# Gate's row by transfers, into the weights of the last projection's second half, and shift columns in one operand: a change to a hybrid decoder layer

## The chip, the cores and the metric

The kernel runs on 1 core of a Trainium2 chip. A core has five engines with instruction queues of their own: TensorE (PE in the profile; its loads of stationary operands are PEld), VectorE (DVE), ScalarE (ACT), GpSimd (POOL) and SyncE (SP); the last two serve here mostly to issue transfers (DMAs). The metric is the device time of one execution in microseconds (us), lower is better.

## The reference

One sequence of 256 rows of 1024 features goes through one hybrid layer. Cut to what matters:

```python
mod = silu(c) @ ada_w + ada_b                       # nine rows of 1024
sh1, sc1, g1, sh2, sc2, g2, sh3, sc3, g3 = split(mod, 9)
u = modulate(rms_norm(h, norm_ffn1_w), sh1, sc1)    # x * (1 + scale) + shift
h = h + 0.5 * g1 * swiglu(u, ffn1_w_in, ffn1_w_out) # (silu(u @ w_gate) * (u @ w_up)) @ w_out
u = modulate(rms_norm(h, norm_mix_w), sh2, sc2)
h = h + g2 * hybrid_mixer(u, ...)                   # state space branch + retention, gated merge
u = modulate(rms_norm(h, norm_ffn2_w), sh3, sc3)
h = h + 0.5 * g3 * swiglu(u, ffn2_w_in, ffn2_w_out) # inner width 2816
return rms_norm(h, norm_final_w)
```

The change touches three things in it: `u` at the entry of the mixer and of the second SwiGLU (its shift), the row `0.5 * g3`, and the product with `ffn2_w_out` that the row multiplies.

## The kernel before

**Products.** Features lie on the 128 partitions and the 256 rows (T) along the columns, until the last projection, which is computed with the rows on the partitions. Every operand of a product is kept as two halves, `hi` (rounded to a shorter float) and `lo` (what is left over), and each fp32 product is three matmuls: hi·hi, hi·lo and lo·hi (`mm3`, L146 to L154, in the profile as L152, L153 and L154, or as L148 to L150 in a turned order).

**Weights.** `load` fetches 1 MB of weights through SP's queue into one of four stage tiles `wst`. `half` (L132 to L139) makes the two halves of 1024 columns in one of four tiles `wh`: ScalarE casts (L137), VectorE subtracts (L138). A stage tile is free for the fourth load after it once its last subtraction is done, a `wh` tile once its last matmul is done. So there is a chain from load to cast to subtraction to the first matmul that reads the low half (L154, where weights stand on the stationary side; L153 in the last projection, where they are the moving operand).

**Early projections.** Twice, at the entry of the mixer and of the second SwiGLU, `modulated` (L265) starts the next product through `early_project` before the rms factor and its application are done: the factor (`rs`, by `rstd`) is made while matmuls run on operands that lack it, and the four results are multiplied by it afterwards (L281). The shift can't go that way. It stands as extra columns T and T + 1 in the operand tiles `uh` and `ul` (written by `shift()` in `residual`), so that the products are 258 columns wide, and column T of each result is the bias that the shift makes; it is copied to `eb` (L280, 128x1). In the second SwiGLU the first result goes with that bias into a silu on ScalarE (L186 on `proj,eb`), and VectorE multiplies with the other (L975). Meanwhile TensorE goes on with the next 256 columns, whose weights are `wh_7775` and `wh_7802` in the order below.

**Second SwiGLU.** Eleven steps of 256 inner features fill `ah` and `al`, the halves of the activations. In the sixth, VectorE makes `g` (L987, 128x8: gate's 1024 numbers, eight to a partition) and a tile of eight diagonals (`diag`, L989). Two fp32 products of `diag` with ones (L993) spread the row over all partitions, and ScalarE copies it to `gb` (L995), 128x1024.

**Last projection.** Two passes of 512 output columns; each has six loads of up to four inner tiles, eleven `wh` tiles, and works for both row tiles (`ps[0]`, `ps[1]`). After pass 0 `gated` multiplies each result by the row (L1011), adds the residual stream `hN` (L1012), squares with a running sum on ScalarE (L1014) and multiplies by the final norm's weight (L1015). Pass 1 keeps its last six inner tiles: what stands in `ps[1]` is multiplied and added first (L1037, L1038), then row tile 0 is finished, then row tile 1 in two pieces of 256 columns, with `gated` after each. The last piece's square, the square root, the reciprocal (L1054), the scaling (L1061 on VectorE, L1063 on ScalarE) and the transfer to DRAM come after the last matmul.

What order the instructions have on each engine is set by a scheduler of the compiler's tile framework; only the mixer's part is written out in an order by hand (the strings of step names). A change of one instruction's form can therefore move others.

Of the kernel before, what the change touches and what calls it, by code (L numbers as in the profile page):

```python
# [18 lines left out]
P = 128  # L19
T = 256  # L20
# [62 lines left out]
def layer(ctx: ExitStack, tc: tile.TileContext, a, out, packing):  # L83
# [57 lines left out]
    def split_into(hi, lo, src):  # L141
        cast = act.copy(hi, src).ins  # L142
        dve.tensor_tensor(lo, src, hi.bitcast(F32), ALU.subtract)
        return cast

    def mm3(o, l, r, first, last, skip=False, turned=False):  # L146
        if turned:
            pe.matmul(o, l[1], r[0], start=False, stop=False, skip_group_check=skip)  # L148
            pe.matmul(o, l[0], r[0], start=False, stop=False, skip_group_check=skip)  # L149
            pe.matmul(o, l[0], r[1], start=False, stop=False, skip_group_check=skip)  # L150
            return
        pe.matmul(o, l[0], r[0], start=first, stop=False, skip_group_check=skip)  # L152
        pe.matmul(o, l[0], r[1], start=False, stop=False, skip_group_check=skip)  # L153
        pe.matmul(o, l[1], r[0], start=False, stop=last, skip_group_check=skip)  # L154

    def at(pair, *idx):
        return pair[0][idx], pair[1][idx]

    def wide_at(u, kt):
        return u[2][:, kt, :], u[3][:, kt, :]  # L160

    al = slice(None)

# [69 lines left out]

    def new_u():
        full = [sp.tile([P, KD, U_ROW], F32R, tag=n, name=nm(n), bufs=1) for n in ("uh", "ul")]
        return tuple(t[:, :, :T] for t in full) + tuple(t[:, :, :T + 2] for t in full)

    def u_tile(u, f, t, jsh):
        sh = modc[:, jsh, f:f + 1]
# [25 lines left out]
    def modulated(ha, u, jsh, w, cols, at_kt=1, c_next=None):  # L265
        rs = []
        ps = early_project(w, cols, u, at_kt, lambda: rs.append(rstd(sums, mean_m)))
        rs = rs[0]
        if c_next is not None:
            st = load(w, 0, KD, c_next, 256)  # L270
            ready.append(half(st[:, :, :P]))
        for f in range(KD):
            t = ha(f)
            dve.tensor_tensor(t, t, rs, ALU.mult)
            u_tile(u, f, t, jsh)
        if c_next is not None:
            ready.append(half(st[:, :, P:]))
        b = sp.tile([P, 4], F32, tag="eb", name=nm("eb"), bufs=1)
        for i in range(4):
            dve.tensor_copy(b[:, i:i + 1], ps[i][:, T:T + 1])  # L280
            dve.tensor_tensor(ps[i][:, :T], ps[i][:, :T], rs, ALU.mult)  # L281
        return [(ps[i][:, :T], b[:, i:i + 1]) for i in range(4)]

    def early_project(w, cols, u, at_kt, between):
        sts = [load(w, 0, KD, c0, 256) for c0 in cols]
        ps = [proj_ps().rearrange("p f t -> p (f t)") for _ in range(2)]
        ps += [misc_ps() for _ in range(2)]
        for kh in range(2):
            hv = [half(st[:, 4 * kh:4 * kh + 4, :]) for st in sts]
            for kk in range(4):  # L290
                kt = 4 * kh + kk
                if kt == at_kt:
                    between()
                for i in range(2):
                    for f in range(2):
                        mm3(ps[2 * i + f][:, :T + 2], at(hv[i], al, kk, slice(f * P, (f + 1) * P)),
                            wide_at(u, kt), kt == 0, kt == KD - 1)
        return ps

    def pair_halves(w, c0):  # L300
# [20 lines left out]
    def residual(jg, factor, am, ha, u, jsh):  # L321
        g = sp.tile([P, KD], F32, tag="g", name=nm("g"), bufs=2)
        dve.tensor_scalar(g, modc[:, jg, :], factor, None, ALU.mult)

        def shift():
            split_into(u[2][:, :, T:], u[3][:, :, T:],
                       modc[:, jsh, :].unsqueeze(2).broadcast_to([P, KD, 2]))

        def done(f, ps):
            if f == KD - 2:  # L330
                shift()
            dve.scalar_tensor_tensor(h[:, f, :], ps, g[:, f:f + 1], h[:, f, :], ALU.mult, ALU.add)
            square_add(f)
            act.activation(ha(f), h[:, f, :], AF.Copy, scale=am[:, f:f + 1])
            act.activation(u[0][:, f, :], h[:, f, :], AF.Copy, scale=am[:, f:f + 1])
            dve.tensor_tensor(u[1][:, f, :], ha(f), u[0][:, f, :].bitcast(F32), ALU.subtract)
        return done
# [626 lines left out]
    with tc.tile_pool(name=nm("fp"), bufs=1, reuse_waits="tile") as fp:  # L964
# [5 lines left out]
        for p2 in range(NF // 2):  # L970
            if p2 == 0:
                s = fp.tile([P, 2, T], F32, tag="s", name=nm("s"), bufs=2)
                for f in range(2):
                    lookup(s[:, f, :], first[f][0], AF.Silu, bias=first[f][1])
                    dve.scalar_tensor_tensor(s[:, f, :], first[2 + f][0], first[2 + f][1],  # L975
                                             s[:, f, :], ALU.add, ALU.mult)
                split_into(ah[:, 0:2, :], alo[:, 0:2, :], s)
            else:
                pg = pair_project(w1, p2 * 256, u, ready if p2 == 1 else None)
                pu = pair_project(w1, FFN + p2 * 256, u)  # L980
                swiglu(fp, pg, pu, ah, alo, 2 * p2)
            ada_next()
            if p2 == 1:
                nc.sync.dma_start(wf, a["norm_final_w"].broadcast_to([P, D]))
            if p2 == 5:
                g = sp.tile([P, KD], F32, tag="g", name=nm("g"), bufs=2)
                dve.tensor_scalar(g, modc[:, 8, :], 0.5, None, ALU.mult)  # L987
                diag = fp.tile([P, KD, P], F32, tag="diag", name="diag")
                dve.tensor_tensor(diag, ident.unsqueeze(1).broadcast_to([P, KD, P]),  # L989
                                  g.unsqueeze(2).broadcast_to([P, KD, P]), ALU.mult)  # L990
                for q in range(2):
                    ps = misc_ps()
                    pe.matmul(ps, ones, diag[:, 4 * q:4 * q + 4, :].rearrange("p f t -> p (f t)"),  # L993
                              start=True, stop=True)
                    act.copy(gb[:, q * 512:(q + 1) * 512], ps)  # L995
            if p2 == 6:
                for tt in range(2):
                    for q in range(2):
                        ps = misc_ps()
                        for f in range(4):  # L1000
                            pe.transpose(ps[:, f * P:(f + 1) * P],
                                         h[:, q * 4 + f, tt * P:(tt + 1) * P], ident)
                        act.copy(hN[:, tt, q * 512:(q + 1) * 512], ps)
# [3 lines left out]
        def gated(tt, ps, c0, n, i):  # L1007
            cs_ = slice(c0, c0 + n)
            t = fp.tile([P, 512], F32, tag="t", name=nm("t"), bufs=2)[:, :n]
            o = hN[:, tt, cs_]  # L1010
            dve.tensor_tensor(t, ps, gb[:, cs_], ALU.mult)  # L1011
            dve.tensor_tensor(t, o, t, ALU.add)  # L1012
            q = fp.tile([P, 512], F32, tag="q", name=nm("q"), bufs=1)[:, :n]
            act.activation(q, t, AF.Square, accum_out=ss[:, tt, i:i + 1])  # L1014
            dve.tensor_tensor(o, t, wf[:, cs_], ALU.mult)  # L1015

        for bi in range(2):
            c0, per, split = bi * 512, 4, NF - 6 if bi else NF
            ps = [proj_ps().rearrange("p f t -> p (f t)") for _ in range(2)]
            hvs = []  # L1020

            def product(o, tt, kt, part, first, last):
                mm3(o, at((ah, alo), al, kt, slice(tt * P, (tt + 1) * P)),
                    at(hvs[kt // 2], al, kt % 2, part), first, last)

            for k0 in range(0, NF, per):
                kn = min(per, NF - k0)
                st = load("ffn2_w_out", k0 * P, kn, c0, 512)
                hvs += [half(st[:, k2:k2 + 2, :], "alike") for k2 in range(0, kn, 2)]
                for kt in range(k0, min(k0 + kn, split)):  # L1030
                    for tt in range(2):
                        product(ps[tt], tt, kt, al, kt == 0, kt == (split if tt else NF) - 1)
            if not bi:
                for tt in range(2):
                    gated(tt, ps[tt], 0, 512, 0)
        t = fp.tile([P, 512], F32, tag="t", name=nm("t"), bufs=2)
        dve.tensor_tensor(t, ps[1], gb[:, 512:], ALU.mult)  # L1037
        dve.tensor_tensor(hN[:, 1, 512:], hN[:, 1, 512:], t, ALU.add)  # L1038
        for tt, q in ((0, None), (1, 0), (1, 1)):
            part = al if q is None else slice(q * T, (q + 1) * T)  # L1040
            o = ps[0] if q is None else proj_ps()[:, 0, :]
# [69 lines left out]
```

## Time and profile before

| | us |
|---|---|
| median of 3 runs | 828.91 (828.78 to 828.99) |
| profiled execution | 828.89 |
| its span in the trace | 826.8 |
| TensorE busy | 816.1 |
| VectorE busy | 666.9 |
| ScalarE busy | 511.0 |
| GpSimd busy | 10.3 |

The granted TensorE clock was 0.998 over the span. The profile comes from one execution: the span is what the trace covers, and 2.1 us lie around it. In rows of the timeline the columns are start, duration, engine, line, operation, output and inputs, the tile's shape and the count; in square brackets stands how long the engine was idle before, and what released it. A matmul's duration includes its way through the array, so matmuls overlap, and the distance from one start to the next is what one costs. Consecutive rows of one kind are joined into one with a count. Rows from the chain that ended last have start, duration, engine, tile and line.

### The profile page before, as it was taken

Reading aid. Unit: us, or ns where it says so; the run is one execution under the profiler, and the core shown is the slowest. Engines: PE = TensorE matmul, PEld = TensorE weight load, DVE = VectorE, ACT = ScalarE, POOL = GpSimd, SP = SyncE. Lnnn points to the kernel's source line nnn. Section 1 sums busy time; section 2 is a strip of 40 time slices with the busy share of each in tenths; the row PEclk is TensorE's granted clock in tenths of the full one; section 3 lists DMA queues with packets and bytes.
Section 4 is the critical chain, followed back from the end, with each engine's and each line's share of the span. In section 5 each row is a group of like instructions: output and inputs, shape, how many; then the busy total and the mean of one; then the engine's idle time right before and its main releaser. Section 6 shows DMA issues by size and latency. Waiting matters only on the chain.

```text
span 826.8 us, 15886 instructions
## 1 busy us (share of the span) xinstructions
PE 816.1 (99%) x6612; PEld 787.0 (95%) x6612; DVE 666.9 (81%) x999; ACT 511.0 (62%) x731; POOL 10.3 (1%) x21
## 2 busy tenths in 40 slices
PE   8999999999999999999999999999999999999996
PEld 7999999999999989999999999999999999999885
DVE  7999899977989988787898778977979985455464
ACT  6566454556898777765565569765568754545342
POOL 0000000000200010000000000000000000000000
PEclk9999999999999999999999999999999999999999
DMA  9998899855685465546657754654565695455521
GB/s 367 415 418 344 314 349 366 335 180 173 233 309 200 158 216 187 200 130 239 229 182 301 254 205 153 211 198 171 212 218 183 255 360 185 176 185 185 206 87 52
DMA packets 30299, 193.08 MB, mean 234 GB/s; under 512 B 3458, under 2 KB 4098, under 8 KB 9619
## 3 DMA queue, kind: packets, MB, share of 16 engines
q1 hardware_dynamic: 28370, 186.07, 61.6%
q0 software_dynamic: 1568, 5.28, 1.9%
q8 instruction: 52, 0.85, 0.4%
q10 hardware_dynamic: 288, 0.72, 0.3%
q14 instruction: 21, 0.16, 0.1%
HBM read 190.97 MB, written 1.08 MB: 232 GB/s over the span
## 4 chain that ended last, share of the span: by engine, by line
PE 90%; ACT 3%; DVE 3%; DMA 3%; issue 1%; SPq 0%; ACTq 0%
PE proj L154 25%; PE proj L153 25%; PE proj L152 25%; PE proj L149 2%; PE proj L150 2%; PE proj L148 2%; DMA wst<-in_ffn_w_in_dram 2%; ACT wh L411 1%; DMA ada<-in_ada_w_dram 1%; PE misc L754 1%; PE misc L898 1%; PE misc L223 1%; DVE wh L414 1%; DVE wh L138 1%; DVE ada L197 1%; PE misc L764 1%
## 5 line engine op out<-in xcount | busy, mean ns | idle before, releaser
L138 DVE TENSOR_TENSOR wh<-wst,wh 128x1024 fp32r<-128x1024 f32 (+1 forms) x262 | 316.8, 1213 | 108.4 <-ACT wh L137 107.5
L137 ACT CAST wh<-wst 128x1024 fp32r<-128x1024 f32 (+1 forms) x262 | 272.4, 1042 | 171.0 <-PE proj L154 132.2
L152 PE MATMUL proj<-uh,wh 128*128 128x256 f32 (+1 forms) x1096 | 304.5, 278 | 0.0
L153 PE MATMUL proj<-ul,wh 128*128 128x256 f32 (+1 forms) x1096 | 303.2, 277 | 0.0
L154 PE MATMUL proj<-uh,wh 128*128 128x256 f32 (+1 forms) x1096 | 303.2, 277 | 0.0
L153 PEld LDWEIGHTS proj<-ul,wh 128*128 128x128 f32 x1096 | 205.8, 188 | 0.4 <-issue 0.2
L152 PEld LDWEIGHTS proj<-uh,wh 128*128 128x128 f32 x1096 | 205.8, 188 | 0.3 <-ACT wh L137 0.2
L154 PEld LDWEIGHTS proj<-uh,wh 128*128 128x128 f32 x1096 | 205.8, 188 | 0.2 <-issue 0.2
L152 PE MATMUL proj<-s,wh 128*128 128x256 f32 x312 | 87.1, 280 | 0.2 <-ACT s L142 0.2
L154 PE MATMUL proj<-s,wh 128*128 128x256 f32 x312 | 86.4, 277 | 0.0
L153 PE MATMUL proj<-s,wh 128*128 128x256 f32 x312 | 86.2, 277 | 0.0
L152 PEld LDWEIGHTS proj<-s,wh 128*128 128x128 f32 x312 | 58.5, 188 | 0.6 <-ACT s L142 0.4
L153 PEld LDWEIGHTS proj<-s,wh 128*128 128x128 f32 x312 | 58.6, 188 | 0.2 <-issue 0.2
L154 PEld LDWEIGHTS proj<-s,wh 128*128 128x128 f32 x312 | 58.6, 188 | 0.0
L197 DVE SCALAR_TENSOR_TENSOR ada<-ada,cb 128x1024 f32<-128x1024 f32 x48 | 57.3, 1219 | 0.0
L148 PE MATMUL proj<-uh,wh 128*128 128x256 f32 x152 | 42.0, 276 | 0.0
L149 PE MATMUL proj<-uh,wh 128*128 128x256 f32 x152 | 42.0, 276 | 0.0
L150 PE MATMUL proj<-ul,wh 128*128 128x256 f32 x152 | 42.0, 276 | 0.0
L152 PE MATMUL proj<-ah,wh 128*128 128x256 f32 x152 | 42.0, 276 | 0.0
L153 PE MATMUL proj<-al,wh 128*128 128x256 f32 x152 | 42.0, 276 | 0.0
L154 PE MATMUL proj<-ah,wh 128*128 128x256 f32 x152 | 42.0, 276 | 0.0
L186 ACT ACTIVATE s<-proj 128x512 f32<-128x512 f32 x33 | 19.7, 598 | 34.6 <-PE proj L154 32.5
(274 smaller groups left out, 1372.8 us busy)
## 6 DMA issues: line engine op xcount, KB each, us to landing
wst<-in_mix_w_in_dram SPq DMA_DIRECT2D x52, 1024.0 KB, 4.9
wst<-in_ffn_w_in_dram SPq DMA_DIRECT2D x43, 1024.0 KB, 5.5
wst<-in_ffn_w_out_dram SPq DMA_DIRECT2D x18, 1024.0 KB, 4.9
ada<-in_ada_w_dram SPq DMA_DIRECT2D x16, 1024.0 KB, 8.4
wst<-in_ada_w_dram SPq DMA_DIRECT2D x12, 1024.0 KB, 5.0
ada<-in_ada_w_dram SPq DMA_DIRECT2D x16, 512.0 KB, 12.6
wst<-in_w_br_ssd_dram SPq DMA_DIRECT2D x8, 1024.0 KB, 5.0
wst<-in_w_br_ret_dram SPq DMA_DIRECT2D x8, 1024.0 KB, 4.9
```

The source lines that it names most:

```text
L137: act.copy(hi, v)
L138: dve.tensor_tensor(lo, v, hi.bitcast(F32), ALU.subtract)
L148: pe.matmul(o, l[1], r[0], start=False, stop=False, skip_group_check=skip)
L149: pe.matmul(o, l[0], r[0], start=False, stop=False, skip_group_check=skip)
L150: pe.matmul(o, l[0], r[1], start=False, stop=False, skip_group_check=skip)
L152: pe.matmul(o, l[0], r[0], start=first, stop=False, skip_group_check=skip)
L153: pe.matmul(o, l[0], r[1], start=False, stop=False, skip_group_check=skip)
L154: pe.matmul(o, l[1], r[0], start=False, stop=last, skip_group_check=skip)
L186: phase["uses"].append(act.activation(*args, **kw).ins)
L197: dve.scalar_tensor_tensor(st[:, i, :], st[:, i, :], 1.0, cb, ALU.mult, ALU.mult, accum_out=raw[:, j, f0 + i:f0 + i + 1])
L223: pe.matmul(ps[:, :T], mean, s, start=i == 0, stop=i == len(parts) - 1)
L411: act.copy(hw[0][j], wst[kt][:, j, :])
```

## The change

Three things, all in the second half of the kernel but for the first of two early projections:

1. Both halves of the shift go into the high operand: hi into column T of `uh`, lo into column T + 1. A new helper, `mm3_shifted`, multiplies 258 columns in the first and the third matmul and 256 in the second. The bias is the sum of two columns of each result, so the copy becomes a reduction.
2. Gate's row is no longer made by TensorE. Two transfers on GpSimd's queue write `g` to DRAM (1024 elements of 4 bytes, each to its place) and read it back to all partitions.
3. In pass 1 of the last projection VectorE multiplies each stage tile of weights by the row's second half, in place, before it is split; what `gated` and the piece before it multiplied there, falls away.

```diff
+    def mm3_shifted(o, l, u, kt, first, last):
+        pe.matmul(o[:, :T + 2], l[0], u[2][:, kt, :], start=first, stop=False)
+        pe.matmul(o[:, :T], l[0], u[1][:, kt, :], start=False, stop=False)
+        pe.matmul(o[:, :T + 2], l[1], u[2][:, kt, :], start=False, stop=last)
...
-            dve.tensor_copy(b[:, i:i + 1], ps[i][:, T:T + 1])
+            dve.tensor_reduce(b[:, i:i + 1], ps[i][:, T:T + 2], mybir.AxisListType.X, ALU.add)
...
-                        mm3(ps[2 * i + f][:, :T + 2], at(hv[i], al, kk, slice(f * P, (f + 1) * P)),
-                            wide_at(u, kt), kt == 0, kt == KD - 1)
+                        mm3_shifted(ps[2 * i + f], at(hv[i], al, kk, slice(f * P, (f + 1) * P)),
+                                    u, kt, kt == 0, kt == KD - 1)
...
-            split_into(u[2][:, :, T:], u[3][:, :, T:],
-                       modc[:, jsh, :].unsqueeze(2).broadcast_to([P, KD, 2]))
+            split_into(u[2][:, :, T], u[2][:, :, T + 1], modc[:, jsh, :])
...
-                diag = fp.tile([P, KD, P], F32, tag="diag", name="diag")
-                dve.tensor_tensor(diag, ident.unsqueeze(1).broadcast_to([P, KD, P]),
-                                  g.unsqueeze(2).broadcast_to([P, KD, P]), ALU.mult)
-                for q in range(2):
-                    ps = misc_ps()
-                    pe.matmul(ps, ones, diag[:, 4 * q:4 * q + 4, :].rearrange("p f t -> p (f t)"),
-                              start=True, stop=True)
-                    act.copy(gb[:, q * 512:(q + 1) * 512], ps)
+                grow = dp.tile([1, KD, P], F32, name="grow")
+                nc.gpsimd.dma_start(grow.rearrange("o f p -> p (o f)"), g)
+                nc.gpsimd.dma_start(gb.rearrange("p (f q) -> p f q", f=KD),
+                                    grow.broadcast_to([P, KD, P]))
...
-            dve.tensor_tensor(t, ps, gb[:, cs_], ALU.mult)
-            dve.tensor_tensor(t, o, t, ALU.add)
+            if i == 0:
+                dve.tensor_tensor(t, ps, gb[:, cs_], ALU.mult)
+                ps = t
+            dve.tensor_tensor(t, o, ps, ALU.add)
...
                 st = load("ffn2_w_out", k0 * P, kn, c0, 512)
+                if bi:
+                    dve.tensor_tensor(st, st, gb[:, 512:].unsqueeze(1).broadcast_to([P, kn, 512]),
+                                      ALU.mult)
...
-        t = fp.tile([P, 512], F32, tag="t", name=nm("t"), bufs=2)
-        dve.tensor_tensor(t, ps[1], gb[:, 512:], ALU.mult)
-        dve.tensor_tensor(hN[:, 1, 512:], hN[:, 1, 512:], t, ALU.add)
+        dve.tensor_tensor(hN[:, 1, 512:], hN[:, 1, 512:], ps[1], ALU.add)
```

The scheduler moves instructions of VectorE at two places. The first is the end of the second early projection. `proj_7538`, `proj_7539` (gate) and `misc_7540`, `misc_7541` (up) are the four results, `rs_7575` the rms factor, `wh_7775` and `wh_7802` the next weight halves, `s_7712` the activations. Before:

```order
L280 COPY eb_7693<-proj_7538 128x1
L280 COPY eb_7693<-proj_7539 128x1
L280 COPY eb_7693<-misc_7540 128x1
L281 TENSOR_TENSOR proj_7538<-proj_7538,rs_7575 128x256
L281 TENSOR_TENSOR proj_7539<-proj_7539,rs_7575 128x256
L281 TENSOR_TENSOR misc_7540<-misc_7540,rs_7575 128x256
L280 COPY eb_7693<-misc_7541 128x1
L138 TENSOR_TENSOR wh_7775<-wst_7772,wh_7775 128x1024
L281 TENSOR_TENSOR misc_7541<-misc_7541,rs_7575 128x256
L975 SCALAR_TENSOR_TENSOR s_7712<-misc_7540,eb_7693,s_7712 128x256
L975 SCALAR_TENSOR_TENSOR s_7712<-misc_7541,eb_7693,s_7712 128x256
L138 TENSOR_TENSOR wh_7802<-wst_7772,wh_7802 128x1024
```

The same place after the change (L280, L281 and L975 of before are L282, L283 and L976 now):

```order
L282 TENSOR_REDUCE eb_7693<-proj_7538 128x1
L282 TENSOR_REDUCE eb_7693<-proj_7539 128x1
L283 TENSOR_TENSOR proj_7538<-proj_7538,rs_7575 128x256
L283 TENSOR_TENSOR proj_7539<-proj_7539,rs_7575 128x256
L282 TENSOR_REDUCE eb_7693<-misc_7540 128x1
L282 TENSOR_REDUCE eb_7693<-misc_7541 128x1
L283 TENSOR_TENSOR misc_7540<-misc_7540,rs_7575 128x256
L283 TENSOR_TENSOR misc_7541<-misc_7541,rs_7575 128x256
L976 SCALAR_TENSOR_TENSOR s_7712<-misc_7540,eb_7693,s_7712 128x256
L976 SCALAR_TENSOR_TENSOR s_7712<-misc_7541,eb_7693,s_7712 128x256
L138 TENSOR_TENSOR wh_7775<-wst_7772,wh_7775 128x1024
L143 TENSOR_TENSOR al_7708<-s_7712,ah_7707 128x512
```

The subtraction for `wh_7775` has moved from behind the third multiplication to behind the fourth and both multiplications with the silu. On ScalarE the casts and the two silus around it stand in the same order as before.

The second place is VectorE's change from pass 0 to pass 1 of the last projection. Before, `wh_9119` is the last weight tile of pass 0, `wh_9150`, `wh_9153` and `wh_9182` are the first three of pass 1, and `t_9134` and `t_9140` belong to the gated results of pass 0:

```order
L138 TENSOR_TENSOR wh_9119<-wst_9117,wh_9119 128x1024
L138 TENSOR_TENSOR wh_9150<-wst_9148,wh_9150 128x1024
L138 TENSOR_TENSOR wh_9153<-wst_9148,wh_9153 128x1024
L138 TENSOR_TENSOR wh_9182<-wst_9180,wh_9182 128x1024
L1011 TENSOR_TENSOR t_9134<-proj_8955,gb 128x512
L1011 TENSOR_TENSOR t_9140<-proj_8956,gb 128x512
...
L1015 TENSOR_TENSOR hN<-t_9140,wf 128x512
L138 TENSOR_TENSOR wh_9185<-wst_9180,wh_9185 128x1024
```

After the change the same tiles have the numbers 9114 (last of pass 0), 9146, 9149 and 9179; L1029 is the new multiplication, on the stage tiles of the first four loads of pass 1, and the gated lines are L1009 to L1014:

```order
L1029 TENSOR_TENSOR wst_9143<-wst_9143,gb 128x2048
L138 TENSOR_TENSOR wh_9082<-wst_9080,wh_9082 128x1024
L138 TENSOR_TENSOR wh_9085<-wst_9080,wh_9085 128x1024
L1029 TENSOR_TENSOR wst_9176<-wst_9176,gb 128x2048
L138 TENSOR_TENSOR wh_9114<-wst_9112,wh_9114 128x1024
L138 TENSOR_TENSOR wh_9146<-wst_9143,wh_9146 128x1024
L1029 TENSOR_TENSOR wst_9209<-wst_9209,gb 128x2048
L138 TENSOR_TENSOR wh_9149<-wst_9143,wh_9149 128x1024
L1029 TENSOR_TENSOR wst_9242<-wst_9242,gb 128x2048
L1009 TENSOR_TENSOR t_9129<-proj_8950,gb 128x512
...
L138 TENSOR_TENSOR wh_9179<-wst_9176,wh_9179 128x1024
```

Four multiplications and the whole of the gated pass 0 now stand ahead of the subtraction for the third weight tile, `wh_9179`; before, `wh_9182` stood ahead of the gated pass.

More of the change, by code (lines that the diff above doesn't have):

```diff
@@ L157, in at @@
         return pair[0][idx], pair[1][idx]
-    def wide_at(u, kt):
-        return u[2][:, kt, :], u[3][:, kt, :]
+    def mm3_shifted(o, l, u, kt, first, last):
+        pe.matmul(o[:, :T + 2], l[0], u[2][:, kt, :], start=first, stop=False)
+        pe.matmul(o[:, :T], l[0], u[1][:, kt, :], start=False, stop=False)
+        pe.matmul(o[:, :T + 2], l[1], u[2][:, kt, :], start=False, stop=last)
     al = slice(None)
@@ L235, in new_u @@
         full = [sp.tile([P, KD, U_ROW], F32R, tag=n, name=nm(n), bufs=1) for n in ("uh", "ul")]
-        return tuple(t[:, :, :T] for t in full) + tuple(t[:, :, :T + 2] for t in full)
+        return tuple(t[:, :, :T] for t in full) + (full[0][:, :, :T + 2],)
     def u_tile(u, f, t, jsh):
```

## Prediction

> **What bounds the kernel now.** I read the page first: the busy shares, then the chain that ended last.
>
> ```profile
> span 826.8 us, 15886 instructions
> PE 816.1 (99%) x6612; PEld 787.0 (95%) x6612; DVE 666.9 (81%) x999; ACT 511.0 (62%) x731; POOL 10.3 (1%) x21
> PE 90%; ACT 3%; DVE 3%; DMA 3%; issue 1%; SPq 0%; ACTq 0%
> ```
>
> TensorE is busy for 99% of the span and carries 90% of the chain. So two things are worth time: matmul time taken off TensorE, and work in the last microseconds, after the last matmul, where the chain leaves TensorE. Work on VectorE (81%) costs nothing until a matmul waits for it. I therefore read the timeline at four places: the gate row's matmuls, the two early projections, the change from the first to the second pass of the last projection, and the end. The sum is made against the profiled execution, 828.89 us (span 826.8 and 2.1 around it), which is the median of the runs (828.91) to 0.02.
>
> **Gate row's matmuls.** TensorE's timeline, where gate's row is made:
>
> ```profile
> 702.01 0.28 PE L154 MATMUL proj<-uh,wh 128*128 128x256 f32 x1
> 702.13 1.88 PE L993 MATMUL misc<-diag,ones 128*128 128x512 f32 x4
> 703.44 0.68 PE L152 MATMUL proj<-uh,wh 128*128 128x256 f32 x1
> 703.96 0.28 PE L153 MATMUL proj<-ul,wh 128*128 128x256 f32 x1
> ```
>
> And the spacing of ordinary matmuls, 256 columns wide and, in the early projection, 258 wide:
>
> ```profile
> 653.11 0.28 PE L152 MATMUL proj<-uh,wh 128*128 128x256 f32 x1
> 653.33 0.28 PE L154 MATMUL proj<-uh,wh 128*128 128x256 f32 x1
> 658.43 0.28 PE L154 MATMUL proj<-uh,wh 128*128 128x256 f32 x1
> 640.34 0.28 PE L152 MATMUL proj<-uh,wh 128*128 128x258 f32 x1
> 647.37 0.28 PE L154 MATMUL misc<-uh,wh 128*128 128x258 f32 x1
> ```
>
> From 653.11 to 658.43 there are 47 steps in 5.32 us: 0.1132 us each. From 702.01 to 703.96 there are two ordinary steps (to L152, to L153), 0.23 us; the other 1.95 − 0.23 = 1.72 us is the gate row. The row's own busy time, 1.88, is the other end. I take **−1.8** (−1.72 to −1.9): TensorE is the bound on both sides of the place, so the time is saved whole. The two ScalarE copies and VectorE's diagonal go too, at nothing, since neither engine is waited for there.
>
> In their stead stand two transfers by GpSimd's queue. Nearest rows, VectorE at the making of g, and the same queue in the mixer:
>
> ```profile
> 675.15 0.17 DVE L987 TENSOR_SCALAR g<-modc 128x8 f32<-128x8 f32 x1
> rows<-m POOLq DMA_DIRECT2D x1, 32.0 KB, 1.9
> m<-rows POOLq DMA_DIRECT2D x5, 512.0 KB, 11.4
> ```
>
> A write of 32 KB to DRAM took 1.9 us and a read of 512 KB from there 11.4 us. With g there at 675.3, gb would be there at about 689 by these rows. Its first reader, the first multiplied weight tile, runs at about 773.6 (below). So 84 us cover it: **0**. Were the cover gone, the 13 us would stand on the path. One end remains: the write here is 1024 elements of 4 bytes and may take far longer than 1.9 us; even 80 us would be hidden. Weights' transfers beside it may land later by its bytes' share; the half tiles ahead on VectorE hide that.
>
> The Trainium skill, "DMA: Bandwidth & Descriptors", section "Rules for kernel authors", speaks against just this write: where the last dimension isn't contiguous, a transfer becomes one descriptor per element, and one should rearrange. By that rule there are 1024 descriptors here, which is the transfers' half of the third rival; no row of before shows such a write.
>
> **Shift columns.** In each of the two early projections the middle matmul of each product narrows from 258 to 256 columns, 32 of 96. The 258 wide ones take 7.03 us for 59 steps, 0.1192, so 5.9 ns more than the 256 wide: 32 × 5.9 = 0.19 us each. But most of those columns come after the rms factor's matmuls, or after which VectorE's chain from the factor to the next operand decides. In the first I take −0.1 (0 to −0.2). In the second 8 matmuls of the 32 stand ahead of the factor, and the rest is eaten by the wait of the next part: −0.05 (0 to −0.1). Sum **−0.15** (0 to −0.3).
>
> The Trainium skill, "TensorE: Matmul & The Clock Gate", section "Back-to-back issue gap", gives a warm gap of N/2.4 + 2.5 ns, so 0.8 ns for two columns, and an estimate of 0.05 us for all 64. This trace's 5.9 ns differs and decides; by the page the total would be 0.1 us later.
>
> **The bias, and what moves behind it.** Summing two columns needs a reduction where a copy stood. VectorE and ScalarE after the second early projection:
>
> ```profile
> 649.90 0.22 DVE L280 COPY eb<-proj 128x1 f32<-128x1 f32 x2
> 650.03 0.15 DVE L280 COPY eb<-misc 128x1 f32<-128x1 f32 x1
> 650.10 0.75 DVE L281 TENSOR_TENSOR proj<-proj,rs 128x256 f32<-128x256 f32 x2
> 650.76 0.42 DVE L281 TENSOR_TENSOR misc<-misc,rs 128x256 f32<-128x256 f32 x1
> 651.09 0.15 DVE L280 COPY eb<-misc 128x1 f32<-128x1 f32 x1
> 651.16 1.22 DVE L138 TENSOR_TENSOR wh<-wst,wh 128x1024 fp32r<-128x1024 f32 x1
> 652.29 0.43 DVE L281 TENSOR_TENSOR misc<-misc,rs 128x256 f32<-128x256 f32 x1
> 652.62 0.87 DVE L975 SCALAR_TENSOR_TENSOR s<-misc,eb,s 128x256 f32<-128x256 f32 x2
> 653.41 1.22 DVE L138 TENSOR_TENSOR wh<-wst,wh 128x1024 fp32r<-128x1024 f32 x1
> 651.87 0.47 ACT L186 ACTIVATE s<-proj,eb 128x256 f32<-128x256 f32 x1
> ```
>
> The subtraction at 651.16 makes the low half of wh_7775, done at 652.38; TensorE uses it first in the L154 at 653.33 (quoted above). So it has 0.95 us to spare. The new order sets it behind the last multiplication (0.33, the step from 650.76 to 651.09) and both L975 (0.40 each, from 652.62 to 653.41). The second L975 needs ScalarE's second silu, whose end, 651.87 + 0.47 = 652.34, hardly moves, since what it waits for stays at its place on ScalarE. So: second L975 at 652.36, subtraction at 652.75, done at 653.97, that is 0.64 after it is needed, or 0.67 with the gap to the matmul. Here TensorE waits where it did not: I take **+0.6** (0.5 to 0.9), a few hundredths being won back where TensorE waits a little today. A reduction of two elements isn't in the trace: no less than the copy's step (0.065, half of the 0.13 from 649.90 to 650.03), and at the other end 0.5 us, above the 0.42 of a 256 wide operation. Four at 0.065 lie in time before the silu; I take the copy's, as the size is nearest to it. At 0.2 each nothing moves beyond 0.3 us; at 0.5 the stall is about 1.9.
>
> **Weights multiplied in the second pass.** VectorE around the pass change, the shapes' means, the loads and the matmul that matters:
>
> ```profile
> L138 DVE TENSOR_TENSOR wh<-wst,wh 128x1024 fp32r<-128x1024 f32 x20 | 24.4, 1225 | 23.2 <-ACT wh L137 23.2
> L1012 DVE TENSOR_TENSOR t<-hN,t 128x512 f32<-128x512 f32 x2 | 1.3, 683 | 0.0
> wst<-in_ffn_w_out_dram SPq DMA_DIRECT2D x5, 1024.0 KB, 4.8
> 768.21 26.77 SPq L118 DMA_DIRECT2D wst<-in_ffn_w_out_dram  x6
> 788.66 1.23 DVE L138 TENSOR_TENSOR wh<-wst,wh 128x1024 fp32r<-128x1024 f32 x1 [1.49 <-ACT wh L137]
> 789.80 1.28 DVE L1011 TENSOR_TENSOR t<-proj,gb 128x512 f32<-128x512 f32 x2
> 793.41 2.36 DVE L138 TENSOR_TENSOR wh<-wst,wh 128x1024 fp32r<-128x1024 f32 x2
> 787.58 1.05 ACT L137 CAST wh<-wst 128x1024 fp32r<-128x1024 f32 x1 [1.67 <-PE proj L154]
> 795.77 0.39 PE L153 MATMUL proj<-wh,ah 128*128 128x512 f32 x1
> ```
>
> A multiplication of 512 takes 0.683 and one of 1024 1.225, so 0.54 per 512 and 2.3 us for 2048. Six of them (five of 2048, one of 1024) are 12.7 us of VectorE, whose idle in this stretch was 23.2 us: it holds if the order is right. I step through it. Subtractions ran every 2.72 us (matmul pace), each 1.1 after its cast. VectorE is free at 773.6, and the second pass's first load, issued at 768.21, has landed at 773.0. First multiplication to 775.9; two subtractions of pass 0 (the second waits for its cast, 777.8) to 778.95; second multiplication to 781.2; the last of pass 0 to 782.35, whose buffer is the fourth load's, issued so at 782.4 and landed at 787.2; the first half tile of pass 1 waits for its cast, 783.2, to 784.4; third multiplication to 786.7; second half tile to 787.85; fourth multiplication to 790.1; the gated pass 0 (789.80 to 793.41 today: 3.6) to 793.7; the third half tile's low half to 794.85. Today this one was done at 789.9; TensorE needs it at 795.77. So 0.9 us is left: **0**. After that each load needs 2.3 + 2 × 1.15 = 4.6 of 5.44 us. If the margin goes, it costs what is over; I bound it by +1.2.
>
> **The end.** TensorE's last matmul, VectorE and ScalarE:
>
> ```profile
> 820.13 0.28 PE L154 MATMUL proj<-wh,al 128*128 128x256 f32 x1
> 820.46 0.16 DVE ss L1047
> 820.53 0.42 DVE L1011 TENSOR_TENSOR t<-proj,gb 128x256 f32<-128x256 f32 x1
> 820.99 0.42 DVE L1012 TENSOR_TENSOR t<-hN,t 128x256 f32<-128x256 f32 x1
> 821.51 0.42 ACT L1014 ACTIVATE q<-t 128x256 f32<-128x256 f32 x1 [1.08 <-DVE t L1012]
> ```
>
> With L1011 gone the addition starts where the product is there, 820.45, and ends at 820.87; the two small sums come earlier, as the multiplications ahead are gone. The square starts at 820.93, for 821.51: **−0.58** (−0.5 to −0.6), and all behind it moves along. The earlier multiplications that go (L1037, the 512 wide L1011) lay beside matmuls: 0.
>
> **Sum:** −1.8 − 0.15 + 0.6 + 0 − 0.58 = −1.93; 828.89 − 1.93 = 827.0. Its own range goes from 828.9 − 1.9 − 0.3 + 0.5 − 0.6 = 826.6 to 828.9 − 1.72 + 0.9 − 0.5 = 827.6.
>
> **Rivals.**
> 1. The wait at 653.33 does not come, because the reordered subtraction finds a gap, or TensorE regains it later: the 0.6 is off, 826.4. For: after it VectorE is often idle. Against: the chain through the silu above. 0.17.
> 2. The margin of 0.9 is used up (a load lands later, a cast waits), and TensorE waits at the third half tile by about 1: 828.0. For: four multiplications lie ahead of it. Against: the steps give 794.85. 0.13.
> 3. The reduction takes 0.5 us, or the write of single elements holds the weights' transfers: the gain is nearly gone, 827.0 + 1.3 = 828.3. 0.13.
> 4. Slower: VectorE becomes the bound of the second pass, because a multiplication in place on 2048 takes twice the price, 4.4 us. The same steps then put the first multiplication's end at 778.0, pass 0's last at 785.85, the third multiplication's at 791.4, the fourth's at 796.95 and the low half at 801.7: 5.9 late, 832.9. It decides from 2.7 us a multiplication on, since the last two then delay the low half by 2 × 0.43. Against: every row of VectorE here goes at 0.54 per 512. 0.06.
>
> **How the numbers follow.** The forecast has 0.51, the rivals as given. The range 826.2 to 828.6 holds the forecast and rivals 1, 2 and 3; rival 4 and the edges are left out. About 0.2% (1.66 us, so 827.25 on the fast side) is what can be told from no change. Faster by more: rival 1 and 0.8 of the forecast, 0.58. Within: the rest of it, rivals 2 and 3, and a little of 4's smaller forms, 0.35. Slower: 0.07.
>
> **What would show it.** Right: no L993; L153 0.23 us after the L154 before it; TensorE waiting about 0.6 for VectorE's L138 near 653; multiplications of 2.3 us; no wait in the pass change; the last square about 0.5 us after the last matmul's end. Wrong: a gap at the third half tile, reductions far over 0.07, or the first multiplication waiting for gb.

## The result and the profile after

The changed kernel takes 826.18 us (median of 7 runs, 825.93 to 826.43) against 828.83 (828.66 to 828.99): ratio 0.9968, interval 0.9957 to 0.9979, so 2.65 us faster. Forecast were 1.9 and a range from 826.2: the direction was right, and the time lies 0.02 below the range. That 0.02 is less than the runs scatter; what has to be explained is 2.65 where 1.9 was forecast. The page of the changed kernel:

```profile
span 824.2 us, 15888 instructions
PE 814.2 (99%) x6608; PEld 785.6 (95%) x6608; DVE 675.1 (82%) x1000; ACT 509.8 (62%) x729; POOL 11.7 (1%) x23
PE 88%; DVE 4%; ACT 3%; DMA 3%; issue 1%; SPq 0%; ACTq 0%
```

TensorE's busy time fell by 1.9 and the span by 2.6; VectorE's rose by 8.2. Where the 2.6 us came from is read by laying the two traces side by side. For the same cast of weights on ScalarE, the start before less the start in the changed kernel, in us (medians over 10 us; the last column is ScalarE's last square):

| at (us of before) | 0 | 50 to 190 | 210 | 280 to 570 | 590 to 640 | 670 to 690 | 710 to 770 | 820 |
|---|---|---|---|---|---|---|---|---|
| earlier by | 0.0 | 0.14 | 0.20 | 0.48 | 0.77 | 0.20 | 2.05 | 2.59 |

The places of the prediction are the steps at 195 to 280, 640 to 670, 700 and 820; the change of passes shows none. The steps at 50 and at 580 lie where nothing was changed; the next section shows that they belong to the execution.

**Gate's row.** TensorE's timeline where L993 was:

```profile
700.00 0.28 PE L153 MATMUL proj<-ul,wh 128*128 128x256 f32 x1
700.12 0.28 PE L154 MATMUL proj<-uh,wh 128*128 128x256 f32 x1
700.23 0.28 PE L152 MATMUL proj<-uh,wh 128*128 128x256 f32 x1
700.34 0.28 PE L153 MATMUL proj<-ul,wh 128*128 128x256 f32 x1
```

GpSimd's queue, with the write and the read:

```profile
676.81 0.91 POOL L990 DMA_DIRECT2D grow<-g  x1 [347.51 <-DVE g L988]
689.52 0.56 POOL L991 DMA_DIRECT2D gb<-grow  x1 [11.80 <-DMA grow<-g]
```

And the issue of the read on the page of transfers, with KB and us from issue to landing:

```profile
gb<-grow POOLq DMA_DIRECT2D x1, 512.0 KB, 8.7
```

L153 is 0.22 us behind the L154 ahead of it, as with no row between. The read was issued 12.7 us after the write of the single elements, and took 8.7: gb is there at about 698, later than the 689 that the nearest rows gave, and still 73 us ahead of its first reader at 771.4.

**First early projection.** Behind it, small matmuls (L681 before, L682 now) wait for VectorE's `av`, the end of its chain from the rms factor. TensorE there, before:

```profile
216.37 0.28 PE L152 MATMUL proj<-uh,wh 128*128 128x256 f32 x1
216.48 0.28 PE L153 MATMUL proj<-ul,wh 128*128 128x256 f32 x1
216.85 0.63 PE L681 MATMUL misc<-av,k 128*128 128x32 f32 x4
```

And in the changed kernel:

```profile
216.28 0.28 PE L153 MATMUL proj<-ul,wh 128*128 128x256 f32 x1
216.39 0.28 PE L154 MATMUL proj<-uh,wh 128*128 128x256 f32 x1
216.50 0.28 PE L152 MATMUL proj<-uh,wh 128*128 128x256 f32 x1
216.64 0.63 PE L682 MATMUL misc<-av,k 128*128 128x32 f32 x4
```

`av` comes 0.21 us earlier, 0.14 of which the trace has had since 50 us: VectorE's chain keeps the narrower matmuls' gain down to 0.07. But before, 0.26 us were lost ahead of L681 (0.37 from 216.48 for 0.11), and now two more ordinary matmuls stand ahead of the group, which fill 0.23 of it. That is where the table goes from 0.20 to about 0.48. The traces of the experiments below bear this out: the two matmuls stand ahead of the group, and casts get 0.2 to 0.35 us earlier there, wherever the bias is a reduction, also in the kernel in which no matmul is narrowed; with the copy there are neither.

**Second early projection.** VectorE of the changed kernel:

```profile
649.11 0.22 DVE L282 TENSOR_REDUCE eb<-proj 128x1 f32<-128x2 f32 x2
649.30 0.76 DVE L283 TENSOR_TENSOR proj<-proj,rs 128x256 f32<-128x256 f32 x2
650.83 0.47 DVE L976 SCALAR_TENSOR_TENSOR s<-misc,eb,s 128x256 f32<-128x256 f32 x1
651.58 0.48 DVE L976 SCALAR_TENSOR_TENSOR s<-misc,eb,s 128x256 f32<-128x256 f32 x1 [0.28 <-ACT s L188]
651.99 1.22 DVE L138 TENSOR_TENSOR wh<-wst,wh 128x1024 fp32r<-128x1024 f32 x1
```

TensorE of the same kernel, where the low half is read first:

```profile
652.44 0.28 PE L153 MATMUL proj<-ul,wh 128*128 128x256 f32 x1
652.56 0.28 PE L152 MATMUL proj<-uh,wh 128*128 128x256 f32 x1
652.67 0.28 PE L153 MATMUL proj<-ul,wh 128*128 128x256 f32 x1
653.25 0.39 PE L154 MATMUL proj<-uh,wh 128*128 128x256 f32 x1 [0.31 <-DVE wh L138]
653.48 0.28 PE L152 MATMUL proj<-uh,wh 128*128 128x256 f32 x1
```

A reduction of two elements costs 0.095 us on the mean (two in the 0.19 from 649.11 to 649.30). The second L976 waits for the silu, the subtraction is done at 653.21, and L154 waits for it, as forecast. The scheduler had also set two matmuls of the next tile (652.56 and 652.67) ahead of the waiting one, which the prediction had not looked at; they fill 0.23 us. L154 comes at 653.25 where 652.78 would follow, and the next at 0.23 for 0.11 behind it: 0.59 us lost.

**Change of passes.** VectorE of the changed kernel:

```profile
771.44 2.28 DVE L1029 TENSOR_TENSOR wst<-wst,gb 128x2048 f32<-128x2048 f32 x1
785.70 2.28 DVE L1029 TENSOR_TENSOR wst<-wst,gb 128x2048 f32<-128x2048 f32 x1
787.90 1.28 DVE L1009 TENSOR_TENSOR t<-proj,gb 128x512 f32<-128x512 f32 x2
791.51 4.62 DVE L138 TENSOR_TENSOR wh<-wst,wh 128x1024 fp32r<-128x1024 f32 x4
```

TensorE at the third half tile:

```profile
793.50 0.39 PE L152 MATMUL proj<-wh,ah 128*128 128x512 f32 x1
793.72 0.39 PE L153 MATMUL proj<-wh,ah 128*128 128x512 f32 x1
```

A multiplication of 2048 takes 2.28 us (forecast 2.3). The third half tile's low half is done at 791.51 + 1.22 = 792.73, and L153 reads it at 793.72: 1.0 us to spare, forecast 0.9, and no wait.

**The end.** VectorE's last addition, ScalarE's last square, and the last matmul:

```profile
818.40 0.42 DVE L1011 TENSOR_TENSOR t<-hN,proj 128x256 f32<-128x256 f32 x1 [0.38 <-PE proj L154]
818.92 0.42 ACT L1013 ACTIVATE q<-t 128x256 f32<-128x256 f32 x1 [1.27 <-DVE t L1011]
818.09 0.28 PE L154 MATMUL proj<-wh,al 128*128 128x256 f32 x1
```

From the last matmul to the square there are 0.83 us, before 821.51 − 820.13 = 1.38: 0.55 off.

So the steps came out near their terms but for the first early projection. What the sum lacks was the next question, and there was a second hint: the profiled executions took 828.89 and 825.93 us, 2.96 apart, with spans 2.6 apart. The time of an execution less its span, here called the time around the span, was 2.13 us before and 1.77 after.

### The profile page after: what moved, and what is told of

It reads as the page before. It is cut to its first block, busy times and chain, and to the rows that moved or that the text cites. A ratio compares the mean times of both kernels' runs of the same rounds, so it can differ in the third digit from the quotient of the medians.

```text
span 824.2 us, 15888 instructions
## 1 busy us (share of the span) xinstructions
PE 814.2 (99%) x6608; PEld 785.6 (95%) x6608; DVE 675.1 (82%) x1000; ACT 509.8 (62%) x729; POOL 11.7 (1%) x23
## 4 chain that ended last, share of the span: by engine, by line
PE 88%; DVE 4%; ACT 3%; DMA 3%; issue 1%; SPq 0%; ACTq 0%
PE proj L154 25%; PE proj L153 25%; PE proj L152 25%; PE proj L150 2%; PE proj L148 2%; PE proj L149 2%; DMA wst<-in_ffn_w_in_dram 2%; ACT wh L412 1%; DMA ada<-in_ada_w_dram 1%; PE misc L755 1%; DVE wh L138 1%; PE misc L899 1%; DVE ul L243 1%; DVE wh L415 1%; DVE ada L199 1%
## 5 line engine op out<-in xcount | busy, mean ns | idle before, releaser
L138 DVE TENSOR_TENSOR wh<-wst,wh 128x1024 fp32r<-128x1024 f32 (+1 forms) x262 | 316.3, 1212 | 95.6 <-ACT wh L137 92.7
L152 PE MATMUL proj<-uh,wh 128*128 128x256 f32 x1064 | 294.6, 277 | 0.0
L153 PE MATMUL proj<-ul,wh 128*128 128x256 f32 x1064 | 294.2, 277 | 0.0
L154 PE MATMUL proj<-uh,wh 128*128 128x256 f32 x1064 | 293.9, 276 | 0.3 <-DVE wh L138 0.3
L153 PEld LDWEIGHTS proj<-ul,wh 128*128 128x128 f32 x1064 | 199.8, 188 | 0.5 <-DVE ul L243 0.2
L154 PEld LDWEIGHTS proj<-uh,wh 128*128 128x128 f32 x1064 | 199.7, 188 | 0.5 <-DVE wh L138 0.5
L152 PEld LDWEIGHTS proj<-uh,wh 128*128 128x128 f32 x1064 | 199.8, 188 | 0.0
L154 PE MATMUL proj<-s,wh 128*128 128x256 f32 x312 | 86.3, 277 | 0.0
L153 PE MATMUL proj<-s,wh 128*128 128x256 f32 x312 | 86.2, 277 | 0.0
L153 PEld LDWEIGHTS proj<-s,wh 128*128 128x128 f32 x312 | 58.6, 188 | 0.2 <-issue 0.2
L154 PEld LDWEIGHTS proj<-s,wh 128*128 128x128 f32 x312 | 58.6, 188 | 0.0
L148 PE MATMUL proj<-uh,wh 128*128 128x256 f32 x152 | 42.0, 276 | 0.0
L149 PE MATMUL proj<-uh,wh 128*128 128x256 f32 x152 | 42.0, 276 | 0.0
L150 PE MATMUL proj<-ul,wh 128*128 128x256 f32 x152 | 42.0, 276 | 0.0
L153 PE MATMUL proj<-al,wh 128*128 128x256 f32 x152 | 42.0, 276 | 0.0
L154 PE MATMUL proj<-ah,wh 128*128 128x256 f32 x152 | 42.0, 276 | 0.0
```

What stands on the lines that cost most here:

```text
L138: dve.tensor_tensor(lo, v, hi.bitcast(F32), ALU.subtract)
```

## The experiments

Theory A: the terms hold, and what is missing comes from outside the four places (moved matmuls, their pace, the time around the span). Theory B: the shift columns are worth more than forecast. The first four ran on one chip: the kernel before once more, and each of the three parts alone, taken over as in the change's diff.

**The kernel before, unchanged.**

> The kernel before once more, unchanged. The two traces put 0.6 to 0.7 us of the gain where no term of the prediction has any: the matmuls of before ran at 119 ns instead of 113 in a few stretches, such as 576 to 583 us, and those of after did not. Theory A (the pace belongs to the execution): this trace of the same program shows other stretches at 119 ns, and its span may differ by some tenths. Theory B (the pace belongs to the program): the same stretches, span within 0.1 of 826.8. Either way the time is the same, ratio 1.000 within 0.0004.

828.91 against 828.92, ratio 1.000 (0.9991 to 1.0009). Its profiled execution took 829.65 with a span of 827.5, and all of the 0.7 us by which this is longer had come by 80 us. Around 580 us it does not show the stretch at 118 ns: from 578 to 584 us its matmuls stand 113.7 ns apart on the mean, in the first trace of the same program 117.8. So both steps of the table, at 50 and at 580 us, belong to the execution, not to the program: of the thirteen traces here, seven have 117.5 to 118.5 ns at 580 us and six 113.3 to 113.7, with and without the change, and the two traces of the changed kernel differ there as well (113.3 and 117.5).

**Gate's row by transfers alone.**

```diff
-                diag = ... ; pe.matmul(ps, ones, diag...) ; act.copy(gb...)
+                nc.gpsimd.dma_start(grow.rearrange("o f p -> p (o f)"), g)
+                nc.gpsimd.dma_start(gb..., grow.broadcast_to([P, KD, P]))
```

> The gate row by transfers alone; the row is still multiplied in at the end, shift columns as before. By the sum: 1.8 us faster (1.72 to 1.9), 827.0, with L153 about 0.23 us after the L154 that stood ahead of the removed matmuls, and every other place as before. Rival: the write of single elements holds up the weights' transfers, so that less than 1.5 comes out.

827.14 against 828.92: 1.78 faster, ratio 0.9979 (0.9970 to 0.9988). The term is confirmed. Between the traces the step at this place is 1.85 us, as it is for the changed kernel.

**Weights multiplied alone.**

```diff
+                if bi:
+                    dve.tensor_tensor(st, st, gb[:, 512:].unsqueeze(1)..., ALU.mult)
-            dve.tensor_tensor(t, ps, gb[:, cs_], ALU.mult)      # for i >= 1, and before L1038
```

> The weights of the second pass multiplied by the row alone; the row is made on TensorE as before, shift columns as before. By the sum: 0.58 us faster (0.5 to 0.6), 828.25, all of it behind the last matmul, and no wait in the change of passes. Rival: the margin of 0.9 us there is gone and TensorE waits at the third half tile, so that there is no gain.

827.90: 1.02 faster, ratio 0.9987 (0.9978 to 0.9996). Its span is 826.2, which is 0.58 below that of the first trace, just the term; its time of 827.96 leaves 1.78 around the span. The other 0.4 us lies there.

**Shift columns alone.**

```diff
-                        mm3(ps[2 * i + f][:, :T + 2], ..., wide_at(u, kt), ...)
+                        mm3_shifted(ps[2 * i + f], ..., u, kt, ...)
-            dve.tensor_copy(b[:, i:i + 1], ps[i][:, T:T + 1])
+            dve.tensor_reduce(b[:, i:i + 1], ps[i][:, T:T + 2], mybir.AxisListType.X, ALU.add)
```

> The shift columns alone, gate's row and weights as before. By the sum: 0.15 off for narrower matmuls and 0.6 on for the wait behind the second early projection, so 0.45 slower, 829.3. Rival, if what the trace shows ahead of 583 us belongs to this edit: 0.6 more off, so 0.1 to 0.2 faster, 828.7. In the trace of both: TensorE waits for VectorE's L138 near 652 us.

828.64: 0.28 faster, ratio 0.9996 (0.9988 to 1.0005), so not told from no change. The rival's number came out, but not by the rival's reason alone: the time around the span is 1.79 here too, so in the span this part cost about 0.1, where 0.45 was forecast. Against the first trace of before, casts gain 0.3 us behind the first early projection and lose 0.56 behind the second, where TensorE waits for the subtraction as in the changed kernel; the 0.26 at 580 us that the rival counted on comes and goes with the execution.

The three parts sum to 3.08, more than the whole. Two of them hold the 0.35 around the span, which the whole can have only once: 3.08 − 0.35 = 2.73.

The next four ran together as well.

**The change once more.**

> The changed kernel once more, beside the ones below on one chip. 826.2 and a ratio of 0.9968 within 0.0004. The time of the profiled execution less its span was 2.1 us for before, for its repeat and for the row alone, and 1.75 for the weights alone, the shift columns alone and the changed kernel: if these 0.35 us belong to the program, 1.75 comes again; if to the execution, it may be 2.1.

826.44 against 828.99, ratio 0.9968 (0.9956 to 0.9980). Around the span: 826.44 − 824.56 = 1.88. The low value came again, in all six executions (1.74 to 1.88).

**One reduction for four biases, in the second early projection.**

```diff
-            dve.tensor_reduce(b[:, i:i + 1], ps[i][:, T:T + 2], mybir.AxisListType.X, ALU.add)
+            dve.tensor_copy(e2[:, 2 * i:2 * i + 2], ps[i][:, T:T + 2])
             dve.tensor_tensor(ps[i][:, :T], ps[i][:, :T], rs, ALU.mult)
+        dve.tensor_reduce(b, e2.rearrange("p (i c) -> p i c", c=2), mybir.AxisListType.X, ALU.add)
```

> The changed kernel, but the second early projection copies each result's two shift columns (128x2) and reduces all four in one instruction, behind the multiplications; the scheduler then sets the subtraction for the first weight tile behind up's half ahead of both multiplications with the silu. If TensorE's wait for it, 0.84 us, is the price of the moved subtraction, it goes and the time is 825.4. Rival: the silu and what follows it are later by the subtraction's 1.1 us, and TensorE waits there instead: 826.2 or more.

826.53, ratio 0.9969 (0.9957 to 0.9980): no faster. VectorE of this kernel, where the subtraction is the L138 at 651.61:

```profile
651.54 0.15 DVE L289 TENSOR_REDUCE eb<-e 128x4 f32<-128x8 f32 x1
651.61 1.22 DVE L138 TENSOR_TENSOR wh<-wst,wh 128x1024 fp32r<-128x1024 f32 x1
652.74 0.87 DVE L982 SCALAR_TENSOR_TENSOR s<-misc,eb,s 128x256 f32<-128x256 f32 x2
```

TensorE of this kernel at the first use of that low half, the L154:

```profile
653.10 0.28 PE L152 MATMUL proj<-uh,wh 128*128 128x256 f32 x1
653.21 0.28 PE L153 MATMUL proj<-ul,wh 128*128 128x256 f32 x1
653.32 0.28 PE L154 MATMUL proj<-uh,wh 128*128 128x256 f32 x1
```

The subtraction is done at 652.83, and L154 comes 0.11 us behind the matmul ahead of it: TensorE no longer waits there. Against the first trace of the changed kernel 0.4 us are won between 640 and 670 us. But around the span lay 2.14 us, for 1.81 in the change beside it (medians of six each). So the rival's number came out by a cause that neither expectation had: the wait went, and the time around the span took back what it had cost.

**The middle matmul wide again.** Two columns of zeros in the low operand, written by one more instruction on ScalarE, keep all 96 matmuls at 258.

```diff
-        pe.matmul(o[:, :T], l[0], u[1][:, kt, :], start=False, stop=False)
+        pe.matmul(o[:, :T + 2], l[0], u[3][:, kt, :], start=False, stop=False)
```

> The changed kernel, but the middle one of three matmuls is 258 columns wide as well, over two columns of zeros in the low operand, so that all 96 of an early projection are 258 wide as before. If the narrowing is worth what the two traces show, 0.27 us in the first and 0.25 in the second, 0.5 slower than the changed kernel: 826.7. By the prediction's term 0.15 slower: 826.35. Matmuls 119 ns apart, for 116 with the narrow ones.

826.82, 0.38 above the change on the same chip (ratio to before 0.9973, 0.9962 to 0.9983; the intervals overlap). TensorE of this kernel:

```profile
640.55 0.28 PE L160 MATMUL proj<-uh,wh 128*128 128x258 f32 x1
640.67 0.28 PE L161 MATMUL proj<-ul,wh 128*128 128x258 f32 x1
640.79 0.29 PE L162 MATMUL proj<-uh,wh 128*128 128x258 f32 x1
640.91 0.28 PE L160 MATMUL proj<-uh,wh 128*128 128x258 f32 x1
```

TensorE of the changed kernel at the same place:

```profile
639.86 0.28 PE L160 MATMUL proj<-uh,wh 128*128 128x258 f32 x1
639.98 0.28 PE L161 MATMUL proj<-ul,wh 128*128 128x256 f32 x1
640.10 0.28 PE L162 MATMUL proj<-uh,wh 128*128 128x258 f32 x1
640.21 0.28 PE L160 MATMUL misc<-uh,wh 128*128 128x258 f32 x1
```

Three steps take 0.36 us wide and 0.35 with a narrow one. Over all 96 of a projection the mean is 119 ns wide and 116 with one in three narrow: 0.27 us a projection and not 0.19, so two columns less in one matmul of three took half of the excess off. How much of it reaches the end is less clear: laid beside the trace of the changed kernel on this chip, the wide one loses 0.13 us at the first early projection and 0.09 at the second, 0.2 together. The other 0.2 of the 0.38 is not told from noise.

**Each multiplication of the weights twice.**

```diff
                     dve.tensor_tensor(st, st, gb[:, 512:].unsqueeze(1)..., ALU.mult)
+                    dve.tensor_tensor(st, st, gb[:, 512:].unsqueeze(1)..., ALU.mult)
```

> The changed kernel with every multiplication of the second pass's weights made twice (the results are the row's square times the product; the outputs are not the reference's). A multiplication then takes 4.56 us. By the prediction's steps the margin at the third half tile is 0.9 and the limit 2.7 us a multiplication, so TensorE waits about 6 us in the change of passes: 832. If the margin is much larger than stepped through, as the four buffers decide it, less than 1 us: below 827.2.

829.68: 3.2 slower than the change, ratio to before 1.0009 (1.0000 to 1.0018). Neither 832 nor less than 827.2 came out. Of the 3.2, 0.37 lies around the span (2.18 us for 1.81, medians); the span grew by 2.9. From 772 to 816 us VectorE is busy for 43.57 of 44, in the changed kernel for 33.85. The stretch of this kernel, busy times in the order PE, PEld, DVE, ACT, POOL:

```profile
772.00:816.00 44.00, 42.86 (x190) 34.77 (x189) 43.57 (x34) 15.61 (x18) 0.00 (x0) 1.00 0.32 108
```

The same of the changed kernel:

```profile
772.00:816.00 44.00, 44.00 (x204) 36.80 (x203) 33.85 (x31) 16.99 (x21) 0.00 (x0) 1.00 0.31 108
```

VectorE does become the bound, as in the prediction's fourth rival, but at half the price: the scheduler does not leave both multiplications together, and puts several of the second ones behind the gated pass. TensorE's largest wait by the profile, 0.94 us, is at 807 us and not at the third half tile.

The last three test what the time around the span goes by.

```diff
     dve.memset(epsc, EPS)
+    spare = cst.tile([P, 1], F32, name="spare")
+    dve.memset(spare, 0.0)
```

**The kernel before with one instruction more.**

> The kernel before with one more instruction on VectorE, a 128x1 memset at the start that nothing waits for. The time of a profiled execution less its span is 2.13 to 2.16 us where the trace counts 1208 instructions on VectorE (before, its repeat, the row alone, the copies together), 1.77 to 1.88 where it counts 1209 (weights alone, shift columns alone, the changed kernel twice, the wide one), 2.29 at 1213. Theory A (the place of VectorE's last instructions in its code decides this): 1209, so 0.35 faster, 828.5, with 1.75 to 1.9 around the span. Theory B (it comes from what the edits compute, or by chance): 828.9, with 2.13.

828.62 against 828.92: 0.30 faster, ratio 0.9996 (0.9987 to 1.0005), with 829.09 − 827.30 = 1.79 around the span for 2.13. The interval of the time holds no change, but the quantity itself moved as theory A had it: 1.74 to 1.90 in all eleven executions, 2.09 to 2.25 in the sixteen of before beside them, with the same median span of 826.8.

**The copies together with one instruction more.**

> The copies together (one reduction for four biases) with one more 128x1 memset at the start. Its trace gained 0.4 us after the second early projection, which its time did not show, with 2.14 around the span for 1.8. Theory A: 1209 instructions on VectorE, 1.8 around the span, 826.15, so 0.3 below the changed kernel. Theory B: 826.5.

825.98, ratio 0.9964 (0.9950 to 0.9977), 1.78 around the span: the fastest of all. Beside the changed kernel, 826.18 and 826.44 in the earlier sessions, that is 0.2 to 0.5 less. The fairest partner ran on the same chip: the next kernel, which keeps the wait for the subtraction, has as little around the span and takes 826.40, 0.42 more. So that wait costs 0.4 us of time.

**The change with seven more.**

> The changed kernel with seven more such memsets, 1216 instructions on VectorE, a multiple of eight as 1208 is. Theory A with a period of eight: 2.13 around the span, so 0.3 slower than the changed kernel, 826.75. Theory A with another period, or theory B: 826.4.

826.40, ratio 0.9971 (0.9959 to 0.9982), 1.77 around the span. The count of 1216 belongs to the low group, so a period of eight is out.

## Why the prediction was wrong in its number

| term | forecast | measured | by |
|---|---|---|---|
| gate's row | −1.8 | −1.78 in time, −1.85 at its place | the row alone; both traces at 700 us |
| first early projection | −0.1 | −0.07, and −0.23 by two moved matmuls | both traces at 216 us |
| second, narrowing | −0.05 | about 0 | 0.30 won by 647 us, 0.26 lost by 651 |
| wait for the moved subtraction | +0.6 | +0.59 | the trace after; 0.53 in its repeat |
| weights, change of passes | 0 | 0 | 1.0 us to spare |
| the end | −0.58 | −0.55 | both traces |
| around the span | none | −0.35 | 64 low and 107 high executions, and the extra memset |
| sum | −1.93 | −2.4 to −2.5 | |

1. The step that failed is the first: "The sum is made against the profiled execution, 828.89 us (span 826.8 and 2.1 around it)", and those 2.1 were kept fixed. They are not: the change, two of its three parts alone, and even one added memset move them to 1.8. The prediction had this term at nothing without a reason. With −0.35 the forecast would have been 826.7, and its range of 826.2 to 828.6, moved along, would have held the result.
2. The second is a move on TensorE that the prediction had not read: in the first early projection the term for the narrowing was right (−0.1 forecast, −0.07 found, since VectorE's chain eats the rest), but the scheduler also set two matmuls into the wait behind it, worth −0.23. The narrowing itself was mis-sized, 0.27 us a projection for 0.19, to little effect: VectorE's chain took most of it back in both. In the second, TensorE then loses 0.29 us waiting at 649 us, and 0.1 in the kernel with all matmuls wide.
3. The first rival gives almost the measured time (826.4), but its mechanism did not occur: TensorE loses at the moved subtraction what was forecast. To take the result for it would be wrong; only the copies together show what the time is without that wait, 0.42 less beside a kernel that has it.
4. The fourth rival's mechanism is real, and 2.28 us a multiplication keep it away; its price of 5.9 was too high, 2.9 in the span with each multiplication made twice, as the order was assumed and the scheduler set another.
5. The transfers' half of the third rival did not come, though the write of single elements took 12.7 us to the next issue; the reduction's half neither, at 0.095 us.

So −2.4 to −2.5 is accounted for of −2.55 (the change once more) to −2.65. The rest lies within what repeats of one kernel differ by. What is shown is where the time went; why an instruction on VectorE changes the time around the span stays open.

## What to carry to other kernels

Take the time around the span out of every pair of runs before explaining a difference of some tenths: here one memset that nothing waits for moved it by as much as a real edit. When a change alters the form of an instruction on a busy engine, read the new order on all engines around it: the reduction cost nothing by itself, 0.59 us by what moved on VectorE, and two pairs of matmuls that moved on TensorE won 0.23 us each. Work on an engine that has room is free only while its margin at the tightest step holds, and that margin can be stepped through from the trace: 0.9 forecast, 1.0 found.

## What the runs showed of the hardware

- The device time less the traced span has two values in these runs. With spans read to 0.1 us, it is 2.09 us or more in all 107 executions of four kernels (medians 2.13 to 2.18; three have 1208 traced instructions on VectorE, one has 1213), and 1.71 to 1.92 in all 64 executions of seven others (medians 1.79 to 1.84; six have 1209, one has 1216). One added memset, with its 128x1 tile, changes it from the one to the other in two kernels. Whether it goes by the number of VectorE's instructions, by their place or by the tile isn't shown.
- Between 578 and 584 us the same program runs its matmuls 113 or 118 ns apart, from execution to execution, at a granted clock of 1.00 in both. Transfers don't tell them apart: 127 to 175 GB/s in the six faster stretches, 139 to 161 in the seven slower ones. The cause is open.
- A 256 wide matmul among 258 wide ones shortens mostly the two steps behind it: in the second early projection of the changed kernel the steps are 118.0 ns from a wide one to the narrow one, 115.6 from the narrow to the next wide one and 114.9 between two wide ones, against 119.1 where all are wide.
